# Output gates of a hybrid attention and recurrence block projected in pairs, with the first products of ten pairs moved into the recurrence's stage

## The chip, the cores and the metric

The kernel runs on one core of a Trainium2 chip. The metric is the device time of one execution in microseconds (us), of which the median over three runs is given. The engines are named as in the profile: PE is TensorE's matmul (PEld its weight load), DVE is VectorE, ACT is ScalarE, POOL is GpSimd, and SP is SyncE, which issues the DMA transfers.

## The reference

One layer of an encoder block on a sequence of S = 1024 rows with D = 1024 columns, all in float32. One input projection feeds two mixers; their outputs are merged with gates, and an MLP follows:

```python
proj = x @ w_in
(aq, ak, av, gq, gk, gv, gout, lr_f, lr_b, gate_a, gate_g) = split(proj)
# mixer A: dilated window attention, 3 groups of 4 heads (dilations 1, 4, 16), mixed by their softmax denominators
# mixer B: gated linear attention (GLA), 4 heads, forward and backward over chunks
o_gla = o_gla * rsqrt(mean(o_gla ** 2) + NORM_EPS)
y_gla = o_gla * gla_norm_g * silu(gout)
merged = sigmoid(gate_a) * (y_attn @ w_attn_branch) + sigmoid(gate_g) * (y_gla @ w_gla_branch)
x = layernorm(ALPHA * x + merged @ w_out)
x = layernorm(ALPHA * x + squared_relu(x @ w_ff1 + b_ff1) @ w_ff2 + b_ff2)
```

The part that the change touches is the projection `x @ w_in`. Its columns are cut into 36 blocks of 128 (array `wfm`): 0 to 3 are the recurrence's q and k, 4 to 7 the output gates `gout`, 8 to 23 the two merge gates, 24 to 29 attention's q, 30 to 35 attention's k.

## The kernel before

**Precision.** Every float32 operand is split into a high part, rounded by a copy to the type fp32r, and a low part, the rest. `mm3` (L96) multiplies with three matmuls for each 128 rows of contraction: high by high, high by low, low by high (L100, L101, L102). `load_w` (L87) loads a weight block into a ring of two buffers `raw`, lets ACT make the high part `whi` (L91) and, unless told otherwise, POOL the low part `wlo` (L93). `halve` (L145) does the same for other operands with ACT (L146) and DVE (L147).

**A block alone.** A block of 128 columns times the whole x is two halves of 512 rows, each 8 x 3 = 24 matmuls of 512 columns into one bank of a ring of three (`mmtile`).

**A pair of blocks.** `proj` (L487) computes two blocks at once as a 2 x 2 block product by Winograd's scheme: 7 products of 12 matmuls instead of 8. The sums of x blocks it needs (T1 to T4) are made once by `xsum` (L453) from x loaded anew (`xload`, L448), the sums of weight blocks (S1 to S4) for each pair by `side`. Products are named m1 to m7. m1 (block A11 by B11) leaves its bank as `u2`, a copy by ACT (L547); m2 (A12 by B21) adds to the same bank, which is then the finished first half of the pair's first block; m6, m7, m5, m4, m3 follow, with sums on DVE (L542). Each of the four finished pieces is stored to the DRAM array `spill` by `put` (L519); for attention's q and k this reorders rows by the group's dilation r.

**Order of the stages.** After the start come the recurrence's inputs, and then the recurrence itself: four heads (`gla_head`, L293), each a chain of nine units over PE, ACT, DVE and POOL. `merge_streams` (L58) writes other work between these units: two blocks of q and k, attention's v (`att_v_units`, L422), and the first four half blocks of the output gates (`spill_units`, L403). The other four half blocks stand behind the last head. Then the tiles of the recurrence are given up, T1 to T3 take their place, and T4 takes that of a part of x that is no longer needed. At this handover the sums are made, and between them the products m1 and m2 of the first two pairs run (L618).

After that comes a list of steps, one product each; a step's weight sums are prepared three steps ahead (L816). There are 14 pairs: attention's q and k for groups 2, 1 and 0, then the merge gates. From step 11 on, 27 visits of attention (`visit`, L792) are spread over the steps; the eight `silu` units (L780), which read the stored gates, stand at steps 1 to 8. The merge stage follows, with `load_w` for eight branch weights, and then the output projection, the layer norm and the MLP.

**Who orders the engines.** The program text gives dependencies and priority. A planner in the build (L1546) lays the instructions of each engine in the order in which its own model of time lets them start, earlier text first. On the chip each engine then keeps to that list. So work of different units lies interleaved on PE, and an instruction that is late on the chip holds up what is listed behind it.

## Time and profile before

| What | us |
|---|---|
| median of 3 runs | 1450.34 |
| lowest and highest run | 1446.51 and 1451.52 |
| the profiled execution | 1448.67 |
| its span, first to last instruction | 1446.9 |
| PE busy in it | 1400.9 |
| DVE busy | 994.1 |
| ACT busy | 622.4 |
| POOL busy | 84.6 |

Busy time is the time in which an engine had at least one instruction running. For PE it counts overlapping matmuls once, so it says that the engine was never empty, not how fast it ran. In the rows of the order of time, the first number is the start in us from the span's beginning, the second the duration, then engine, line, operation, output and inputs, and in brackets the idle time before with what ended it. In the rows of waits the three numbers are the total in us, how often, and the longest. In groups, the first number after the bar is the busy time, the second the mean duration in ns. Rows of the windows view give a stretch, its length, the busy time of each engine with the number of instructions, the granted clock of PE, the DMA engines' share and GB/s.

The stages lie about so in the span: start and the recurrence's inputs to 95 us, the four heads to 264 us, the handover to 297 us, the paired projections with attention to 641 us, merge to 710 us, then the rest.

### The profile page before, as it was taken

The numbers are of one execution on the slowest core, as the hardware profiler recorded it, in microseconds if no ns is written. First come the engines' busy times: TensorE is split into PE (matmuls) and PEld (weight loads), VectorE is DVE, ScalarE is ACT, GpSimd is POOL, SyncE is SP. The second block draws the span as 40 slices with busy tenths as digits, with TensorE's granted clock in tenths as the row PEclk, the third lists the DMA queues.
The fourth block names the chain that finished last, engine by engine and source line by source line (L and its number), as shares of the span: only waits on it lengthen the run. The fifth ranks groups of instructions, "written<-read, shape, count | busy, mean of one in ns | idle before, by whom it ended". The sixth has DMA issues, their size and how long they took to land.

```text
span 1446.9 us, 18910 instructions
## 1 busy us (share of the span) xinstructions
PE 1400.9 (97%) x6842; PEld 1167.8 (81%) x6842; DVE 994.1 (69%) x1710; ACT 622.4 (43%) x1180; POOL 84.6 (6%) x67
## 2 busy tenths in 40 slices
PE   8999889989999999999999898999999999999997
PEld 6989887877888888878888676888888888888885
DVE  5155745777555578566646988776666798786988
ACT  5244532434433344345405743555455633433333
POOL 2220312000000000022000000000000000000001
PEclk9999999999999999999999899999999999999999
DMA  7242403495543454275612476854433883544313
GB/s 232 70 132 63 153 31 123 153 280 180 178 144 128 137 165 136 82 231 167 242 58 87 146 243 240 302 170 154 156 139 116 287 331 117 189 131 145 100 47 117
DMA packets 122522, 227.98 MB, mean 158 GB/s; under 512 B 20685, under 2 KB 53709, under 8 KB 122428
## 3 DMA queue, kind: packets, MB, share of 16 engines
q1 hardware_dynamic: 122284, 226.57, 47.4%
q8 instruction: 54, 0.88, 0.3%
q14 instruction: 40, 0.33, 0.1%
q10 hardware_dynamic: 144, 0.20, 0.0%
HBM read 155.32 MB, written 72.44 MB: 157 GB/s over the span
## 4 chain that ended last, share of the span: by engine, by line
PE 86%; DVE 6%; DMA 5%; issue 1%; ACT 1%; SPq 0%; POOL 0%; DVEq 0%; ACTq 0%; POOLq 0%
PE ps L100 16%; PE ps L102 16%; PE ps L101 16%; PE mm L100 10%; PE mm L101 10%; PE mm L102 10%; PE avp L733 3%; DMA x1dr<-res 2%; PE sc L699 2%; PE tr L720 1%; DMA res<-x1dr 1%; PE sc L372 1%; DMA tb<-in_b_ff 1%; DVE T L982 0%; DVE xr L992 0%
## 5 line engine op out<-in xcount | busy, mean ns | idle before, releaser
L93 POOL TENSOR_TENSOR wlo<-raw,whi 128x768 fp32r<-128x768 f32 (+2 forms) x26 | 57.4, 2212 | 505.0 <-ACT whi L91 497.6
L981 ACT CAST T<-hp 128x1024 fp32r<-128x1024 f32 x36 | 37.9, 1052 | 110.0 <-PE ps L101 70.3
L100 PE MATMUL mm<-whi,x 128*128 128x272 f32 (+1 forms) x256 | 81.0, 317 | 0.0
L101 PE MATMUL mm<-wlo,x 128*128 128x272 f32 (+1 forms) x256 | 80.6, 315 | 0.0
L102 PE MATMUL mm<-whi,x 128*128 128x272 f32 (+1 forms) x256 | 80.5, 314 | 0.0
L101 PE MATMUL ps<-B,B 128*128 128x512 f32 x160 | 62.4, 390 | 0.0
L102 PE MATMUL ps<-B,B 128*128 128x512 f32 x160 | 62.3, 389 | 0.0
L100 PE MATMUL ps<-B,B 128*128 128x512 f32 x160 | 61.0, 391 | 0.5 <-ACT B L981 0.5
L100 PE MATMUL ps<-T,fraw 128*128 128x512 f32 x128 | 52.2, 409 | 7.6 <-ACT T L981 5.3
L102 PE MATMUL ps<-B,T 128*128 128x512 f32 x144 | 56.2, 390 | 0.0
L100 PE MATMUL ps<-B,T 128*128 128x512 f32 x144 | 56.2, 390 | 0.0
L102 PE MATMUL ps<-T,T 128*128 128x512 f32 x144 | 56.1, 390 | 0.0
L101 PE MATMUL ps<-T,T 128*128 128x512 f32 x144 | 56.0, 389 | 0.0
L100 PE MATMUL ps<-T,T 128*128 128x512 f32 x144 | 56.0, 389 | 0.0
L101 PE MATMUL ps<-B,T 128*128 128x512 f32 x144 | 56.0, 389 | 0.0
L1360 DVE TENSOR_TENSOR acc<-ps,acc 128x512 f32<-128x512 f32 x68 | 45.8, 689 | 12.9 <-PE ps L102 12.2
L982 DVE TENSOR_TENSOR T<-hp,T 128x1024 fp32r<-128x1024 f32 x36 | 44.0, 1223 | 15.3 <-ACT T L981 15.2
L100 PE MATMUL mm<-x,whi 128*128 128x512 f32 x120 | 47.6, 408 | 6.9 <-ACT x L146 5.8
L709 ACT ACTIVATE e<-e,sm 128x256 f32<-128x256 f32 (+2 forms) x96 | 43.2, 452 | 24.5 <-DVE sm L704 24.4
L101 PE MATMUL ps<-T,fraw 128*128 128x512 f32 x128 | 52.0, 406 | 1.2 <-DVE T L982 1.2
L102 PE MATMUL ps<-T,fraw 128*128 128x512 f32 x128 | 51.5, 404 | 0.0
L542 DVE TENSOR_TENSOR cr<-cu,mm 128x512 f32<-128x512 f32 x42 | 33.7, 805 | 23.2 <-PE mm L102 22.3
(424 smaller groups left out, 4166.5 us busy)
## 6 DMA issues: line engine op xcount, KB each, us to landing
hdr<-c SPq DMA_DIRECT2D x112, 256.0 KB, 2.5
hp<-hdr SPq DMA_DIRECT2D x56, 512.0 KB, 3.7
spill<-cr SPq DMA_DIRECT2D x56, 256.0 KB, 2.6
gate<-spill SPq DMA_DIRECT2D x32, 256.0 KB, 3.0
wa<-in_w SPq DMA_DIRECT2D x16, 512.0 KB, 5.0
wb<-in_w SPq DMA_DIRECT2D x16, 512.0 KB, 6.8
praw<-in_wfm SPq DMA_DIRECT2D x14, 512.0 KB, 4.2
pwhi<-in_wfm SPq DMA_DIRECT2D x14, 512.0 KB, 3.8
```

Of the source, the lines that this page charges most:

```text
L93: (lo_eng or G).tensor_tensor(lo, raw, hi.bitcast(F32), op=OP.subtract)
L100: T.matmul(ps, lh, rh, start=first and i == 0, stop=False, skip_group_check=more)
L101: T.matmul(ps, lh, rl, start=False, stop=False, skip_group_check=more)
L102: T.matmul(ps, ll, rh, start=False, stop=last and i == n - 1, skip_group_check=more)
L372: T.matmul(ap[d][:, i], kd[pr, cs], qd[pr, cs], start=True, stop=True)
L542: V.tensor_tensor(o, a, b, op=OP.add)
L699: T.matmul(sps[i][:, pr, 0:w], q[ps_, pr], k[ps_, pr, 0:w], start=True, stop=True)
L709: issued["exp"] = A.activation(e, e, AF.Exp, bias=sm[:, h:h + 1], scale=-1.0, accum_out=sm[:, 4 + h:5 + h])
L733: T.matmul(av[:, h * 64:h * 64 + 64], b["et"][h % 2][p0:p0 + vv.shape[0], h // 2, j], vv[:, h * 64:h * 64 + 64], start=j == 0, stop=j == n ...
L981: A.copy(o[:, 0], src)
L982: V.tensor_tensor(o[:, 1], src, o[:, 0].bitcast(F32), op=OP.subtract)
L1360: V.tensor_tensor(m, p, m, op=OP.add)
```

## The change

The output gates (blocks 4 to 7) become two more pairs, ahead of the others, so there are 16 pairs and no `spill_units`. For the first ten pairs, m1 and m2 are computed as `first_products`: the first block's weights are loaded whole by `load_w`; the first 12 matmuls give `u2`, which ACT copies and SP stores to a new DRAM array `u2dr`; 12 more accumulate into the same bank, and ACT copies out the finished half, which is stored to `spill`. Eight of the ten stand between the units of the recurrence, two behind. In the steps these ten pairs have five products instead of seven and read `u2` back from DRAM. The products at the handover go. `load_w` uses DVE for the low part everywhere. The ring `stg` gets a fourth buffer, and the `silu` units and attention's visits move behind the first four pairs (`n0` is 20).

```diff
-    def load_w(src, shape, lo_eng=None):
+    def load_w(src, shape):
...
-        (lo_eng or G).tensor_tensor(lo, raw, hi.bitcast(F32), op=OP.subtract)
+        V.tensor_tensor(lo, raw, hi.bitcast(F32), op=OP.subtract)
...
+    u2dr = dr.tile([16, 128, 512], F32, name="u2dr")
...
-    stg = P.open("stg", bufs=3, side="right")
+    stg = P.open("stg", bufs=4, side="right")
...
-    def spill_units(blocks):
...
+    pairs_in = [((b, b + 1), 1) for b in (4, 6)]
+    for g in (2, 1, 0):
+        pairs_in += [((b + 2 * g, b + 2 * g + 1), ORD[g]) for b in (24, 30)]
+    pairs_in += [((b, b + 1), 1) for b in range(8, 24, 2)]
+    NP, EARLY = len(pairs_in), 10
...
+    def first_products(i):
+
+        (b, _), r = pairs_in[i]
+        hi, lo = load_w(io["wfm"][b], [128, KT, 128])
+        w = fm_pairs(hi, lo, 0)
+        ps = mmtile()
+        mm3(ps, w[:4], True, True)
+        o = stg.tile([128, 512], F32, tag="stg", name="u2")
+        A.copy(o, ps)
+        SP.dma_start(u2dr[i], o)
+        mm3(ps, w[4:], False, True, True)
+        o = stg.tile([128, 512], F32, tag="stg", name="h11")
+        A.copy(by_residue(o, r, False), by_residue(ps, r, True))
+        store(b, r, 0, o)
...
-    gout = spill_units(range(4, 8))
-    merge_streams(crit, [lambda: gla_qk("q", 1), lambda: gla_qk("k", 1)] + att_v_units() + gout[:4])
-    for u in gout[4:]:
+    first = [lambda i=i: first_products(i) for i in range(EARLY)]
+    merge_streams(crit, [lambda: gla_qk("q", 1), lambda: gla_qk("k", 1)] + att_v_units() + first[:EARLY - 2])
+    for u in first[EARLY - 2:]:
         u()
...
+        def u2_back():
+            c["u2"] = cu()
+            SP.dma_start(c["u2"], u2dr[n])
+
         s1, s2 = side("S1"), side("S2")
+        if n < EARLY:
+            return dict(raw=raw, steps=[(lambda: (u2_back(), s1(), s2()), [m6]), (side("S3"), [m7]),
+                                        (lambda: None, [m5]), (side("A22"), [m4]), (side("S4"), [m3])])
...
-    for p, n in ((p0, 0), (p1, 0), (p0, 2), (p1, 2)):
-        prep, do = p["steps"][n]
-        prep()
-        for f in do:
-            f()
-    for k in (2, 3):
+    projs[0]["raw"]()
+    projs[1]["raw"]()
+    for k in range(4):
         for nm in ("T1", "T3", "T2", "T4"):
             xsum(nm, k)
+        if k < 2:
+            xload(k + 2)
...
-    a, b = p0["steps"][1], p0["steps"][4]
-    steps = [(a[0], b[1]), p0["steps"][3], (b[0], a[1]), *p0["steps"][5:]] + [p1["steps"][n] for n in (1, 3, 4, 5, 6)]
-    n0 = len(steps)
-    for p in projs[2:]:
-        steps += p["steps"]
+    steps = [st for p in projs for st in p["steps"]]
+    n0 = sum(len(p["steps"]) for p in projs[:4])
...
-        units.setdefault(1 + i, []).append(lambda i=i: silu(i // 2, i % 2))
+        units.setdefault(n0 - 9 + i, []).append(lambda i=i: silu(i // 2, i % 2))
...
-    w = [load_w(io["wo"][1, k2], [128, 2, 512], V) for k2 in range(4)]
+    w = [load_w(io["wo"][1, k2], [128, 2, 512]) for k2 in range(4)]
```

More of the change, by code (lines that the diff above doesn't have):

```diff
@@ L400, in gla_head, with by_residue, store @@
         return units
-    def spill_units(blocks):
-        units = []
-        for wi in blocks:
-            box = {}
-            def half(hf, wi=wi, box=box):
-                if hf == 0:
-                    box["w"] = load_w(io["wfm"][wi], [128, KT, 128])
-                hi, lo = box["w"]
-                ps = mmtile()
-                mm3(ps, fm_pairs(hi, lo, hf))
-                o = stg.tile([128, 512], F32, tag="stg", name="stg")
-                V.tensor_copy(o, ps)
-                SP.dma_start(spill[wi, :, hf * 512:hf * 512 + 512], o)
-            units += [lambda f=half: f(0), lambda f=half: f(1)]
-        return units
+    pairs_in = [((b, b + 1), 1) for b in (4, 6)]
[3 more added lines that the diff above has]
+    NP, EARLY = len(pairs_in), 10
+    def by_residue(a, r, natural):
+        return a.rearrange("p (j c) -> p c j" if natural else "p (c j) -> p c j", c=r)
+    def store(block, r, hf, o):
+        dst = spill[block].rearrange("p (c h j) -> p h c j", h=2, c=r)[:, hf]
+        SP.dma_start(dst, by_residue(o, r, False))
+    def first_products(i):
[11 more added lines that the diff above has]
+        store(b, r, 0, o)
     def att_v_units():
@@ L485, in build, with proj @@
     banks = turns([mmtile() for _ in range(3)], 3)
-    def proj(blocks, r, ahead):
+    def proj(n, ahead):
+        blocks, r = pairs_in[n]
         st, c, ps = {}, {}, {}
@@ L513, in nat, with side @@
         def nat(a):
-            return a.rearrange("p (j c) -> p c j", c=r)
+            return by_residue(a, r, True)
         def stored(a):
-            return a.rearrange("p (c j) -> p c j", c=r)
+            return by_residue(a, r, False)
         def put(f, hf, o):
-            dst = spill[blocks[f]].rearrange("p (c h j) -> p h c j", h=2, c=r)[:, hf]
-            SP.dma_start(dst, stored(o))
-        def side(nm, *ops):
+            store(blocks[f], r, hf, o)
+        def side(nm):
             def f():
@@ L597, in proj @@
                                     (side("S4"), [m3])])
-    todo = []
-    for g in (2, 1, 0):
-        todo += [((b + 2 * g, b + 2 * g + 1), ORD[g]) for b in (24, 30)]
-    todo += [((b, b + 1), 1) for b in range(8, 24, 2)]
-    NP = len(todo)
-    projs = []
-    for i, (bl, r) in enumerate(todo):
-        projs.append(proj(bl, r, (lambda i=i: projs[i + 2]["raw"]()) if i + 2 < NP else None))
-    p0, p1 = projs[:2]
-    p0["raw"]()
-    p1["raw"]()
-    for nm in ("T1", "T3", "T2", "T4"):
-        xsum(nm, 0)
-    xload(2)
-    for nm in ("T1", "T3", "T2", "T4"):
-        xsum(nm, 1)
-    xload(3)
-    for p, n in ((p0, 0), (p1, 0), (p0, 2), (p1, 2)):
-        prep, do = p["steps"][n]
-        prep()
-        for f in do:
-            f()
-    for k in (2, 3):
+    projs = []
+    for i in range(NP):
+        projs.append(proj(i, (lambda i=i: projs[i + 2]["raw"]()) if i + 2 < NP else None))
+    projs[0]["raw"]()
+    projs[1]["raw"]()
+    for k in range(4):
         for nm in ("T1", "T3", "T2", "T4"):
             xsum(nm, k)
+        if k < 2:
+            xload(k + 2)
     P.close("tmp")
@@ L808, in build @@
     for i in range(8):
-        units.setdefault(1 + i, []).append(lambda i=i: silu(i // 2, i % 2))
-    units[n0].append(tiles[0][0]) if n0 in units else units.setdefault(n0, [tiles[0][0]])
+        units.setdefault(n0 - 9 + i, []).append(lambda i=i: silu(i // 2, i % 2))
+    units.setdefault(n0, []).append(tiles[0][0])
     for i in range(3):
```

## Prediction

> **What bounds the kernel now.** I read the page's first two parts, then the windows view by stage, then the waits of PE and the order of time on DVE and POOL where PE waited.
>
> ```profile
> PE 1400.9 (97%) x6842; PEld 1167.8 (81%) x6842; DVE 994.1 (69%) x1710; ACT 622.4 (43%) x1180; POOL 84.6 (6%) x67
> 95.00:264.30 169.30, 158.03 (x952) 143.43 (x950) 95.67 (x136) 68.50 (x160) 35.61 (x24) 0.97 0.28 91
> 264.30:297.00 32.70, 30.22 (x136) 24.69 (x133) 29.41 (x49) 19.08 (x35) 0.00 (x0) 1.00 0.66 203
> 341.00:641.00 300.00, 298.61 (x1597) 244.60 (x1595) 193.65 (x544) 123.79 (x344) 7.39 (x4) 0.99 0.46 146
> ```
>
> The last three rows are the recurrence's stage, the handover to the paired projections, and those projections with attention beside them; their columns are length, PE, PEld, DVE, ACT, POOL, granted clock, DMA share, GB/s. PE is the bound: idle for 1.4 us of the 300, for 2.5 of the 32.7, and for 11.3 only in the recurrence. So what counts is how many matmuls there are, and those few idle places. A matmul's duration is not its cost, because matmuls overlap; the cost is the distance of starts:
>
> ```profile
> 80.42 0.40 PE L100 MATMUL mm<-x,whi 128*128 128x512 f32 x1
> ...
> 97.89 0.40 PE L102 MATMUL mm<-x,wlo 128*128 128x512 f32 x1
> ```
>
> These are the first and last of 78 matmuls without a break: 17.47 us over 77 distances, 0.227 us each, though each is recorded with 0.39. In the Trainium skill, the page "TensorE: Matmul & The Clock Gate", section "Back-to-back issue gap", gives about 131 ns as the sustained spacing at 512 columns. By it the 24 matmuls counted below would be an estimated 3.1 us. The rows decide for 0.227.
>
> The idle places, from the waits of PE in the recurrence (95 to 265 us) and in the handover (265 to 345 us):
>
> ```profile
> PE tr L393 <- DVE on L390: 7.6, 3, 4.6
> PE mm L100 <- ACT stgv L441: 1.1, 1, 1.1
> PE av L382 <- DVE am L374: 1.1, 1, 1.1
> PE sc L303 <- ACT am L373: 0.6, 1, 0.6
> PE tr L338 <- PE tr L393: 0.5, 1, 0.5
> PE sc L303 <- DVE am L374: 0.3, 1, 0.3
> ...
> PE mm L100 <- DVE cu L542: 3.6, 2, 2.5
> ```
>
> Together 11.2 us and 3.6 us. The largest (4.6 us) looks like this on DVE and POOL:
>
> ```profile
> 211.45 2.28 DVE L310 TENSOR_TENSOR_SCAN L<-rmask,zb 64x1024 f32<-64x1024 bf16 x1
> 213.76 2.29 DVE L311 TENSOR_TENSOR_SCAN L<-rmask,zb 64x1024 f32<-64x1024 bf16 x1
> 216.08 0.69 DVE L390 TENSOR_TENSOR on<-av,ss 128x512 f32<-128x512 f32 x1
> ...
> 211.64 2.90 POOL L389 TENSOR_TENSOR ss<-ss,mhalf 128x4 f32<-128x4 f32 x1 [3.34 <-DVE ss L388]
> ```
>
> One head's last norm stands behind the next head's scans, and PE's transposes (L393), queued ahead of ready matmuls, wait for it.
>
> **The change, part by part.**
>
> *Matmuls.* Output gates were 4 blocks x 2 halves x 24 = 192 matmuls; as two pairs of 7 products of 12 they are 168. All else is only moved. So 24 go: 24 x 0.227 = **-5.4 us**. By place: ten first pieces of 24 are 240 where 192 stood in and just behind the recurrence; the 48 of the two pairs' first products at the handover go; the steps fall from 94 to 92.
>
> *Weight splits, POOL to DVE.*
>
> ```profile
> L93 POOL TENSOR_TENSOR wlo<-raw,whi 128x768 fp32r<-128x768 f32 (+1 forms) x10 | 23.3, 2331 | 47.2 <-ACT whi L91 47.2
> ...
> L93 DVE TENSOR_TENSOR wlo<-raw,whi x4: 1225/1226/1227, 722.4 to 730.9; 128x1024 fp32r<-128x1024 f32 x4
> ...
> 150.13 1.84 POOL L93 TENSOR_TENSOR wlo<-raw,whi 128x768 fp32r<-128x768 f32 x1 [23.38 <-ACT whi L91]
> 152.82 1.82 POOL L93 TENSOR_TENSOR wlo<-raw,whi 128x768 fp32r<-128x768 f32 x1 [0.85 <-ACT whi L91]
> ...
> 150.13 1.98 DVE L357 SCALAR_TENSOR_TENSOR S<-S,sm,U 64x128 f32<-64x128 f32 x1
> 152.15 0.74 DVE L360 SCALAR_TENSOR_TENSOR S<-S,sm,U 64x128 f32<-64x128 f32 x2
> 152.92 2.80 DVE L362 TENSOR_TENSOR S<-S,sm 128x1024 f32<-128x1024 f32 x1
> 240.87 1.23 DVE L362 TENSOR_TENSOR S<-S,sm 128x1024 f32<-128x1024 f32 x1
> ```
>
> The same DVE step (L362) takes 2.80 us beside a POOL split and 1.23 alone; the L357 that starts with a POOL split ends with it, at 1.98 us where two of their kind at 152.15 (L360) take 0.74. So DVE pays 1.6 us for a POOL split that meets it, more than the 1.23 us it needs to do one of 1024 columns itself. In 95 to 265 us, ten splits become about 16 (the early pieces double the loads): 16 x at most 1.23 = 20 us on a DVE that is busy 95.67 of 169.30 us, less what the ten meetings cost (0 to 16 us). DVE has room; the recurrence's own chain on it no longer gets the 1.6 us knocks that the planned order did not foresee. New is a wait: a split on DVE stands behind ACT's cast, and the recurrence stands behind the split. I take 4 us off the 11.2 us of stalls, near a third: the scans that carry the largest one stay as they are. Bounds: -11.2 (all go) and +4 (each of the three turns between heads one more split of 1.23 late). Term **-4 us**.
>
> In the Trainium skill, the page "SBUF — State Buffer", section "SBUF: two separate sides", says DVE and GpSimd share a port pair under a lock held for the whole instruction. The rows at 150.13 us agree. By that rule the small power on POOL (L389) stays blocked by DVE's two-input work, of which there is now more; that is rival D.
>
> *More work on ACT, DMA and stores in the recurrence.*
>
> ```profile
> raw<-in_wfm SPq DMA_DIRECT2D x4, 512.0 KB, 4.3
> ...
> L91 ACT CAST whi<-raw 128x768 fp32r<-128x768 f32 (+1 forms) x10 | 9.1, 925 | 9.7 <-issue 3.3 <-DMA raw<-in_wfm 2.5 <-DMA raw<-in_wtv 2.4
> ...
> 225.75 1.05 ACT L91 CAST whi<-raw 128x1024 fp32r<-128x1024 f32 x1 [0.80 <-DMA raw<-in_wfm]
> 278.58 0.58 ACT L547 COPY cu<-mm 128x512 f32<-128x512 f32 x1
> 286.68 0.58 ACT L567 COPY cr<-mm 128x512 f32<-128x512 f32 x1
> ```
>
> A piece asks ACT for 1.05 + 2 x 0.58 = 2.2 us in the 5.4 us of its 24 matmuls; ACT was busy 68.50 of 169.30. Its second half accumulates into the bank that ACT has just copied, so it waits for that copy; three banks and the neighbouring piece cover it. A weight buffer turns over in 4.3 + 1.05 + 1.23 = 6.6 us, two buffers give a piece each 3.3 us, against 5.4 needed: 2.1 us to spare. Each piece adds a load of 512 KB and two stores of 256 KB, about 190 GB/s of its 5.4 us, against 91 GB/s now and 203 in the handover. Term 0, bounds 0 to +5 (half a microsecond for each of ten).
>
> *Handover.* Eight pieces lie between the heads' steps, two behind. Head by head, PE's work in the last head (7 pieces of 5.4 = 38 us plus some 10.5 of its own) equals the 48 us that head takes now (217 to 264 us), so the recurrence should end about where it does. Then the operand sums start:
>
> ```profile
> 264.30:297.00 32.70, 9.96 (x32) 5.89 (x32) 0.00 (x0) 0.00 (x0) 0.00 (x0) 1.00 0.66 203
> L146 ACT CAST xT<-xraw x16: 612/624/632, 265.6 to 287.7; 128x512 fp32r<-128x512 f32 x16
> L147 DVE TENSOR_TENSOR xT<-xraw,xT x16: 685/689/693, 267.0 to 289.0; 128x512 fp32r<-128x512 f32 x16
> ```
>
> The first row is of whi alone: 32 matmuls after 264.3, two of three, so 48 of the gates were left; with the 48 first products, 96 x 0.227 = 21.8 us covered sums that end 25 us later. Now 48 to 96 are left (48 if PE takes all eight pieces first, 240 - 144 = 96 if it runs at today's pace). The sums shrink: four splits and five evacuations leave DVE (9 x 0.6), two weight splits come (2 x 1.2), so some 22 us. PE can also do 27 matmuls (6.1 us) on the first three of four sum slices. Uncovered: 22 - 6.1 - (10.9 to 21.8) = 5 to 0 us; I take 1.6. On the other side stands the 3.6 us wait:
>
> ```profile
> 295.64 0.69 DVE L786 TENSOR_TENSOR et<-et,e 128x512 f32<-128x512 f32 x1 [2.72 <-DMA et<-yodr]
> 296.25 0.68 DVE L542 TENSOR_TENSOR cu<-cu,mm 128x512 f32<-128x512 f32 x1
> ```
>
> A silu unit's product waits 2.72 us for its load, and the sum that PE needs stands behind it. The silu units move to steps 11 to 18, where the DMA crowd of the stage's start is over. Term 1.6 - 3.6 = **-2 us**, bounds -3.6 to +5.
>
> *Steps.* Early pairs have 5 steps with 14 DVE operations instead of 7 with 16; each reads its first sum back:
>
> ```profile
> gate<-spill SPq DMA_DIRECT2D x32, 256.0 KB, 3.0
> 504.00:540.00 36.00, 36.00 (x199) 29.26 (x198) 28.58 (x91) 14.45 (x41) 0.00 (x0) 1.00 0.46 144
> 540.00:576.00 36.00, 36.00 (x208) 29.86 (x207) 29.27 (x94) 16.76 (x48) 0.00 (x0) 1.00 0.49 158
> ```
>
> A transfer of that size lands in 3.0 us and is asked for three steps (8.2 us) ahead. The 27 visits of attention fall on 65 steps instead of 77, 2.41 steps a visit instead of 2.85. At its fullest DVE has 81% now (29.27 of 36); a visit takes about 10.4 us, of which 0.44 x 2.72 = 1.2 us go, and with them about 0.6 us of DVE: 7.8 of 9.2 us, 85%. Still below PE, with less slack: **+1 us**, bounds 0 to +6. The eight splits of the merge stage move to DVE beside 68.58 of 69 us of busy PE: 0.
>
> Sum on the profiled execution: 1448.67 (span 1446.9 and 1.8 around it) - 5.4 - 4 - 2 + 1 = 1438.3. The shown runs' median, 1450.34, is 1.7 above it: **1440 us**.
>
> **Rivals.**
>
> A. *DVE becomes what PE waits for*: splits held up by casts delay the recurrence, and the denser visits delay the steps' sums. For it: 81% already. Against it: 1.4 us idle in 300. It takes the bounds +5 and +6 with no gain elsewhere but the count: 1450.3 - 5.4 + 6 = about 1451, no measurable change. 0.15.
>
> B. *The sums lie bare (slower).* PE takes the pieces wherever the recurrence lets it, and none is left at its end. Then PE waits 25 - 6.1 = 18.9 us at the handover: 1450.3 - 5.4 + 18.9 = 1464. It decides from where 25 - 6.1 - 0.227 n exceeds 5.4, that is under 59 matmuls left if the sums still need 25 us, under 46 if 22. Against it: 96 are left now, and at least 48 are written behind the last head. 0.10.
>
> C. *All stalls of the recurrence go*, with more filling work and a DVE that keeps its planned pace: 1450.3 - 5.4 - 11.2 - 3.6 - 2 for the half clock that follows such gaps = 1428. The clock granted there:
>
> ```profile
> 216.00:252.00 36.00, 33.93 (x178) 27.89 (x179) 19.15 (x30) 11.20 (x26) 11.49 (x5) 0.91 0.35 114
> ```
>
> 0.17.
>
> D. *Only the count stays*: the power on POOL and the norm behind the scans wait as before, no stall goes: 1450.3 - 5.4 = 1445, at the bound of what can be measured. 0.11, half of it on each side.
>
> **How the numbers follow.** The forecast (1434 to 1445) has 0.47. About 0.3% (4.3 us) is what a measurement of this kernel can tell from no change. Faster: 0.47 + 0.17 + 0.05 = 0.69; within: 0.15 + 0.06 = 0.21; slower: 0.10. The range takes in A and C: 1427 to 1452; B is left out.
>
> **What would show it.** PE should have 24 matmuls fewer; POOL no L93; L362 at 1.23 us in every head. The waits of PE for `on` (now L390) should fall from 7.6 us toward 4; over 7.6 speaks for D. An idle place of PE just behind the last transposes of the recurrence, ended by xT's casts or subtracts, is B; its length times 1/0.227 is the cover that lacked. In the steps, waits for cu, cr or the splits of several microseconds are A. The prediction is wrong if the recurrence becomes longer by more than the 48 matmuls it gains.

## The result, and the profile after

The changed kernel takes **1456.91 us** (median of 9 runs) where the kernel before, run beside it, takes 1449.49: a ratio of 1.0051, with a 95% interval of 1.0035 to 1.0067. One run of the changed kernel (2335.68 us, granted clock 0.555) and one of e4 below (1585.57 us, 0.833) are left out of the ratios. The change costs 7.4 us; the forecast was 1440, and its range ended at 1452. The profiled execution took 1456.67 us. The recurrence's lines stand one further down than before: L362 is now L363, L390 is L391, L393 is L394.

The first part of the page, the busy times:

```profile
PE 1406.8 (97%) x6818; PEld 1171.0 (80%) x6818; DVE 1010.4 (69%) x1746; ACT 627.6 (43%) x1184; POOL 24.9 (2%) x41
```

The 24 matmuls are gone (6842 to 6818), and POOL has lost its splits. To see where the time went I cut both spans at the same four places: the recurrence's first matmul (L303, `sc`), its last transposes, attention's first score matmul, the first matmul of the merge. The windows view of the kernel before, cut there:

```profile
79.95:264.30 184.35, 173.08 (x1019) 155.88 (x1017) 105.91 (x144) 77.82 (x174) 38.91 (x26) 0.97 0.31 102
264.30:338.80 74.50, 70.86 (x307) 57.61 (x304) 63.33 (x98) 33.66 (x59) 0.00 (x0) 0.98 0.79 242
338.80:641.60 302.80, 301.04 (x1611) 246.42 (x1610) 196.45 (x552) 125.63 (x346) 7.39 (x4) 0.99 0.46 146
641.60:1446.90 805.30, 781.79 (x3424) 639.59 (x3424) 605.33 (x870) 357.77 (x552) 20.13 (x20) 0.99 0.50 169
```

and of the kernel after:

```profile
80.03:276.68 196.65, 183.41 (x1042) 164.08 (x1040) 109.90 (x155) 88.64 (x190) 10.12 (x14) 0.97 0.37 116
276.68:371.84 95.16, 88.42 (x378) 70.64 (x376) 77.72 (x120) 38.56 (x66) 0.00 (x0) 0.98 0.85 271
371.84:650.60 278.76, 277.15 (x1493) 226.50 (x1492) 187.11 (x544) 114.98 (x327) 0.00 (x0) 0.99 0.49 155
650.60:1454.80 804.20, 782.56 (x3424) 640.65 (x3424) 605.02 (x874) 357.42 (x552) 12.39 (x16) 0.98 0.50 169
```

The recurrence is 12.3 us longer for 24 more matmuls of 512 columns (264 where 240 lay), which cost 24 x 0.227 = 5.4. To compare stages whose work has moved, I take from each length what its big matmuls cost (0.227 us for each of 512 columns; 0.174 for each of 384, the mean distance of their starts at full clock in the kernel before; there are 384 of these in the recurrence, whatever the kernel). What is left, called **excess** below, is the recurrence's own small matmuls, the waits, and the time at half clock. In the recurrence it goes from 63.1 to 70.0 us, at the handover from 6.0 to 10.5, in the steps from 93.7 to 96.6; the part behind is 1.0 us shorter. So +6.9 + 4.5 + 2.9 - 1.0, less 5.4 for the count, is +7.9, the difference of the spans (1446.9 and 1454.8).

Only 2.0 of the recurrence's 6.9 us are idle time of PE: its length less its busy time is 11.3 us before (184.35 - 173.08) and 13.2 after (196.65 - 183.41). In the rest PE is busy, but slower. The clock records show 13.7 us at half clock there where they showed 10.2, and in the kernel after the matmuls of L383 start 0.85 us apart at half clock (220.30, 221.15) where they start 0.45 apart at full clock (214.51, 214.96), so these 3.4 us cost an estimated 1.7. The remaining 3.2 us were not taken apart.

The waits of PE in the kernel after, in the recurrence and at the handover:

```profile
PE tr L394 <- DVE on L391: 7.5, 2, 4.3
PE mm L100 <- ACT stgv L454: 3.6, 1, 3.6
PE mm L100 <- ACT u L426: 1.3, 1, 1.3
...
PE mm L100 <- ACT pwlo L147: 4.1, 2, 2.8
PE mm L100 <- ACT h L430: 1.7, 2, 0.9
PE mm L100 <- ACT u L426: 0.8, 1, 0.8
```

The wait for `on` is still there, 7.5 us where it was 7.6; waits for the copies `u` and `h` are new, and the wait for `stgv` is 3.6 us where it was 1.1. Yet DVE itself is no longer disturbed: the group of the step that took 2.80 us beside a split on POOL is now even in all four heads.

```profile
L363 DVE TENSOR_TENSOR S<-S,sm x4: 1218/1224/1227, 113.6 to 252.5; 128x1024 f32<-128x1024 f32 x4
```

The place with the most idle time is a turn between heads, in the order of time on PE:

```profile
203.82 0.39 PE L100 MATMUL mm<-x,whi 128*128 128x512 f32 x1
...
219.42 1.09 PE L394 MATMUL tr<-ident,on 128*128 128x128 f32 x4 [3.17 <-DVE on L391]
...
225.58 0.39 PE L102 MATMUL mm<-x,wlo 128*128 128x512 f32 x1
230.25 1.09 PE L394 MATMUL tr<-ident,on 128*128 128x128 f32 x4 [4.28 <-DVE on L391]
232.59 0.79 PE L100 MATMUL mm<-x,whi 128*128 128x512 f32 x1 [1.25 <-ACT u L426]
```

on ACT:

```profile
229.00 1.06 ACT L326 ACTIVATE ex<-zb 128x1024 f32<-128x1024 f32 x1
231.38 0.69 ACT L396 ACTIVATE yo<-tr,cols 128x512 f32<-128x512 f32 x1 [1.32 <-PE tr L394]
231.96 0.58 ACT L426 COPY u<-mm 128x512 f32<-128x512 f32 x1
```

and on DVE:

```profile
224.90 2.29 DVE L312 TENSOR_TENSOR_SCAN L<-rmask,zb 64x1024 f32<-64x1024 bf16 x1
227.22 0.17 DVE L389 TENSOR_SCALAR ss<-ss 128x4 f32<-128x4 f32 x1
...
229.41 0.69 DVE L391 TENSOR_TENSOR on<-av,ss 128x512 f32<-128x512 f32 x1 [0.90 <-POOL ss L390]
```

From 203.82 to 225.58 us there are 36 matmuls of the early pieces: three first halves of 12, one in each of the three banks; the third follows the wait of 3.17 us. Then nothing is left to run. The first half is complete at 208 us, but the first copy `u` comes at 231.96, because ACT's list has it behind `yo` (231.38), which waits for the transposes on PE, which wait for DVE's norm, which DVE's list has behind the next head's scans. A bank that takes 24 matmuls before it needs a copy holds twice the work for PE.

This turn was not free before either:

```profile
216.92 1.09 PE L393 MATMUL tr<-ident,on 128*128 128x128 f32 x4 [4.61 <-DVE on L390]
219.16 0.79 PE L100 MATMUL mm<-x,whi 128*128 128x512 f32 x1 [1.15 <-ACT stgv L441]
```

PE idles for 5.8 us there before and for 8.7 after (3.17 + 4.28 + 1.25). So the turn is 2.9 us worse; the recurrence's other waits together are about 1 us shorter.

### The profile page after: what moved, and what is told of

Read it like the earlier page. It is cut to its first block, busy times and chain, and to the rows that moved or that the text cites. A ratio compares the mean times of both kernels' runs of the same rounds, so it can differ in the third digit from the quotient of the medians.

```text
span 1454.8 us, 18923 instructions
## 1 busy us (share of the span) xinstructions
PE 1406.8 (97%) x6818; PEld 1171.0 (80%) x6818; DVE 1010.4 (69%) x1746; ACT 627.6 (43%) x1184; POOL 24.9 (2%) x41
## 4 chain that ended last, share of the span: by engine, by line
PE 71%; DMA 4%; DVE 4%; issue 1%; ACT 1%; DVEq 0%; SPq 0%; ACTq 0%
PE ps L100 16%; PE ps L102 16%; PE ps L101 16%; PE mm L100 6%; PE mm L101 5%; PE mm L102 5%; PE avp L735 3%; PE sc L701 2%; PE tr L722 1%; DMA e<-spill 1%; DMA x1dr<-res 1%; DVE T L982 1%; DMA spill<-cr 1%; DMA tb<-in_b_ff 1%; DVE xr L992 1%
## 5 line engine op out<-in xcount | busy, mean ns | idle before, releaser
L93 DVE TENSOR_TENSOR wlo<-raw,whi 128x1024 fp32r<-128x1024 f32 (+2 forms) x36 | 40.0, 1111 | 68.8 <-ACT whi L91 65.3
L100 PE MATMUL mm<-x,whi 128*128 128x512 f32 x136 | 55.1, 415 | 9.0 <-ACT x L147 4.8
L100 PE MATMUL mm<-xT,pwlo 128*128 128x512 f32 x144 | 58.3, 405 | 4.3 <-ACT pwlo L147 4.1
L100 PE MATMUL ps<-T,fraw 128*128 128x512 f32 x128 | 52.5, 412 | 7.0 <-ACT T L981 5.2
L91 ACT CAST whi<-raw 128x1024 fp32r<-128x1024 f32 (+2 forms) x36 | 34.4, 959 | 57.2 <-PE mm L101 27.9
L101 PE MATMUL mm<-xT,pwlo 128*128 128x512 f32 x144 | 57.2, 397 | 0.0
L102 PE MATMUL mm<-xT,pwlo 128*128 128x512 f32 x144 | 56.5, 393 | 0.0
```

What stands on the lines that cost most here:

```text
L91: A.copy(hi, raw)
L93: V.tensor_tensor(lo, raw, hi.bitcast(F32), op=OP.subtract)
L100: T.matmul(ps, lh, rh, start=first and i == 0, stop=False, skip_group_check=more)
L101: T.matmul(ps, lh, rl, start=False, stop=False, skip_group_check=more)
L102: T.matmul(ps, ll, rh, start=False, stop=last and i == n - 1, skip_group_check=more)
```

## The experiments

Fifteen kernels. "R" is the number of matmuls of 512 columns that lie in the recurrence, "excess" that of recurrence and handover together; ratios are to the kernel before, measured beside each group (medians 1449.6 to 1450.8). The medians are of 4 to 10 runs. e3, e9 and e12 compute another `u2`, and e7 and e8 give other outputs than the kernel after, so these five are read for their times alone.

| run | median us | ratio, 95% | R | excess | steps | behind |
|---|---|---|---|---|---|---|
| before | 1449.49 | 1 | 240 | 69.1 | 93.7 | 805.2 |
| after | 1456.91 | 1.0051 (1.0035 to 1.0067) | 264 | 80.5 | 96.6 | 804.2 |
| e1 | 1456.38 | 1.0035 (1.0021 to 1.0049) | 264 | 77.8 | 97.2 | 804.5 |
| e2 | 1442.07 | 0.9941 (0.992 to 0.9961) | 240 | 69.1 | 92.1 | 799.6 |
| e3 | 1456.69 | 1.004 (1.0023 to 1.0056) | 322 | 78.0 | 97.1 | 804.4 |
| e4 | 1449.61 | 0.9998 (0.9981 to 1.0015) | 264 | 79.5 | 96.7 | 797.4 |
| e5 | 1452.02 | 1.0 (0.9986 to 1.0014) | 192 | 82.4 | 91.6 | 798.8 |
| e6 | 1448.28 | 0.9976 (0.9963 to 0.999) | 240 | 71.8 | 97.4 | 804.7 |
| e7 | 1462.89 | 1.0078 (1.0057 to 1.0099) | 264 | 78.9 | 102.9 | 805.3 |
| e8 | 1461.25 | 1.0072 (1.005 to 1.0095) | 192 | 81.4 | 103.8 | 801.3 |
| e9 | 1448.74 | 0.9987 (0.9972 to 1.0003) | 288 | 80.6 | 94.6 | 800.7 |
| e10 | 1450.68 | 0.9998 (0.9985 to 1.0011) | 240 | 81.4 | 98.8 | 798.5 |
| e11 | 1460.08 | 1.0068 (1.0052 to 1.0084) | 192 | 78.9 | 95.8 | 803.3 |
| e12 | 1445.87 | 0.9972 (0.996 to 0.9985) | 240 | 73.6 | 93.0 | 803.3 |
| e13 | 1447.13 | 0.9986 (0.9973 to 1.0) | 240 | 76.3 | 93.3 | 797.3 |
| e14 | 1453.89 | 1.0013 (0.9998 to 1.0027) | 204 | 80.2 | 95.0 | 803.2 |
| e15 | 1447.94 | 0.9981 (0.9968 to 0.9994) | 252 | 71.6 | 97.1 | 804.5 |

The last four columns come from one profiled execution each. That of e5 lies 3.5 us below its median, that of e10 3.3 above, that of e3 2.3 below, so differences of that size in these columns can belong to the execution.

### The weight splits (e1, e2)

In the kernel after, the splits go back to POOL (e1; those of `w_out` stay on DVE); in the kernel before, all go to DVE (e2).

```diff
 e1, in load_w of after:
-        V.tensor_tensor(lo, raw, hi.bitcast(F32), op=OP.subtract)
+        (lo_eng or G).tensor_tensor(lo, raw, hi.bitcast(F32), op=OP.subtract)
 e2, in load_w of before:
-        (lo_eng or G).tensor_tensor(lo, raw, hi.bitcast(F32), op=OP.subtract)
+        V.tensor_tensor(lo, raw, hi.bitcast(F32), op=OP.subtract)
```

> The changed kernel with the weight splits of load_w back on POOL (those of w_out stay on DVE), nothing else. Theory T (three banks hold first halves whose copies are listed on ACT behind the turn to the last head, so PE runs dry there): about as the changed kernel, 1454 to 1459 us, and PE's idle places between 210 and 235 us stay near 10 us. Rival R1 (the splits on DVE delay the recurrence): 5 us or more less, 1451 or below. Rival R2 (the loss is in the steps, by the moved silu units and the denser attention): as T in time, but the last turn is not what counts.

> The kernel before with all weight splits of load_w on DVE, nothing else. T and R2: within 3 us of the kernel before (1446 to 1452), rather faster, since the DVE steps that met a POOL split (up to 2.80 us) go back to 1.23. R1: slower by 5 us or more, 1454 and up.

Both give the splits nothing. e1 equals the kernel after; but L363 takes 1.23 us in all four heads there too, so no split on POOL meets that step, and it is e2 that decides. e2 is 8.7 us faster than the kernel before beside it, but not where the splits were: its windows for the recurrence, the handover and the part behind the steps are

```profile
80.73:265.27 184.54, 172.84 (x1017) 155.86 (x1016) 107.63 (x156) 78.05 (x174) 12.01 (x14) 0.96 0.32 102
265.27:339.48 74.21, 70.89 (x305) 57.62 (x303) 63.46 (x98) 33.74 (x59) 0.00 (x0) 0.98 0.79 243
...
640.80:1440.30 799.50, 779.37 (x3425) 637.78 (x3423) 604.50 (x875) 357.41 (x552) 12.38 (x16) 0.99 0.50 170
```

The first two rows are those of the kernel before to 0.3 us, with POOL at 12.01 us where it had 38.91; the last is 5.8 us shorter. And its waits of PE there:

```profile
PE tr L393 <- DVE on L390: 9.6, 3, 5.7
```

9.6 us for `on`, against 7.6 before, though L362 takes 1.23 us in all four heads of e2. No split on POOL made the stall at the turns; the rows of the kernel after show the norm behind the next head's scans in DVE's list.

### Where the 5 to 8 us behind the steps come from

In e2 and in e4 (below) nothing of the program text behind the steps differs from a kernel that takes 804 to 805 us there, but for who makes the branch weights' low parts, and that is alike in after and e4. I compared the order of the names and shapes on PE over the last 3424 matmuls. It is the same one in before, after, e1, e3, e6, e7 and e15: 804.2 to 805.3 us. It is a second one in e2, e4 and e5: 797.4 to 799.6. A third one in e11, e12 and e14: 803.2 to 803.3. e8, e9, e10 and e13 each have one of their own (797.3 to 801.3). So the planner lists the output projection and the MLP in another order after an edit far ahead of them, probably since it starts from another state at the end of the steps, and between the first two orders lie 5 to 8 us. The time at half clock does not explain it: among the seven kernels of the first order it runs from 19 to 26 us in that part, and their lengths agree to 1.1 us. Waits of PE in that part are, for instance, in the kernel before around the MLP's first tiles

```profile
PE ps L100 <- DVE c L1126: 1.8, 1, 1.8
PE ps L100 <- ACT fwlo L981: 1.8, 1, 1.8
```

and in e2 in the same stretch

```profile
PE ps L100 <- DVE c L1126: 1.0, 1, 1.0
PE ps L100 <- ACT fwlo L981: 0.9, 1, 0.9
```

This is larger than most of what the experiments test, so from here on the column "excess" is read beside the total.

### The copy in the middle, taken out or moved (e3, e4)

```diff
 e3
-        mm3(ps, w[:4], True, True)
+        mm3(ps, w)
         o = stg.tile([128, 512], F32, tag="stg", name="u2")
         A.copy(o, ps)
         SP.dma_start(u2dr[i], o)
-        mm3(ps, w[4:], False, True, True)
 e4
-        A.copy(o, ps)
+        V.tensor_copy(o, ps)
...
-        A.copy(by_residue(o, r, False), by_residue(ps, r, True))
+        V.tensor_copy(by_residue(o, r, False), by_residue(ps, r, True))
```

> The changed kernel with u2 copied after all 24 matmuls of a piece instead of after 12, so a piece never waits for ACT in its middle and a bank holds 5.4 us of PE's work instead of 2.7 (u2 is then the whole sum, so the three other pieces of these pairs come out otherwise). T: the idle places of the last turn fall from some 10 us to 5 or less, the time by 4 to 7 us, 1450 to 1453. R1 and R2: 1455 to 1458, no change beyond 2 us.

> The changed kernel with both copies of a first piece (u2 and the finished half) on DVE instead of ACT. T, if ACT's list is what holds the banks: 3 to 6 us less than the changed kernel, 1450 to 1454. If DVE at the turn is as tied up by the scans as ACT is by what waits for them: no change within 2 us. R1 (DVE is the short engine): slower, 1459 and up. R2: no change.

With whole pieces (e3) the turn that cost 4.28 us looks like this on PE:

```profile
228.10 0.39 PE L102 MATMUL mm<-x,wlo 128*128 128x512 f32 x1
229.06 0.63 PE L394 MATMUL tr<-ident,on 128*128 128x128 f32 x4 [0.58 <-DVE on L391]
231.43 0.50 PE L100 MATMUL mm<-x,whi 128*128 128x512 f32 x1 [1.74 <-ACT h L429]
```

and on DVE:

```profile
228.24 0.68 DVE L391 TENSOR_TENSOR on<-av,ss 128x512 f32<-128x512 f32 x1
```

From the first piece (203.24 us) to 228.10 there are 72 matmuls, three banks of 24, where the kernel after has 36. The wait for `on` falls from 4.28 to 0.58 us here (in the whole recurrence from 7.5 to 0.6). Of these 3.7 us, 2.5 come from PE, which runs out of work at 228.49 instead of 225.97; 1.2 come from the norm, which is done at 228.92 instead of 230.10, since this listing has it ahead of the scans. So the edit changed the lists as well as the cover. The recurrence's excess falls from 70.0 to 57.9: PE's idle time there from 13.2 to 6.0, and the time at half clock from 13.7 to 3.4 us. But it has taken in 322 matmuls, and the handover has lost that cover:

```profile
79.59:277.27 197.68, 191.72 (x1099) 171.01 (x1098) 113.54 (x160) 90.69 (x193) 9.28 (x14) 0.99 0.41 128
277.27:368.43 91.16, 79.11 (x316) 61.81 (x314) 73.18 (x113) 35.91 (x62) 0.00 (x0) 0.91 0.79 250
```

In the second row PE is busy for 79.11 of 91.16 us. Its waits:

```profile
PE mm L100 <- ACT pwlo L147: 6.7, 1, 6.7
PE mm L101 <- DVE xT L148: 3.3, 2, 1.9
```

The operand sums lie bare, the handover's excess rises from 10.5 to 20.1, and the total stays. e4's seven microseconds are again behind the steps (797.4 against 804.2); its excess is that of the kernel after. Its first copy `u` starts at 232.24 us on DVE, where ACT had it at 231.96: at a turn both engines' lists are full of the head's own chain, so which of them copies does not matter.

### How many pieces lie between the heads (e5, e6)

```diff
-    merge_streams(crit, [lambda: gla_qk("q", 1), lambda: gla_qk("k", 1)] + att_v_units() + first[:EARLY - 2])
-    for u in first[EARLY - 2:]:
+    merge_streams(crit, [lambda: gla_qk("q", 1), lambda: gla_qk("k", 1)] + att_v_units() + first[:4])
+    for u in first[4:]:
```

This is e5; e6 has 6 in the place of 4.

> The changed kernel with four of the ten first pieces written between the recurrence's units and six behind them, instead of eight and two. Theory F (too many pieces stand ahead of the last head's units, and each gives PE only 2.7 us of work before its bank waits for a copy; what is used there is missing as cover of the operand sums): the recurrence ends near 266 us instead of 277, and the time of recurrence and handover beyond their matmuls falls from 80.5 us by 6 or more. Rival H (each turn between heads simply costs what it costs, whatever is written there): recurrence and handover beyond their matmuls stay at 79 or more. The rows behind the merge are listed as in e2 and e4, where that part took 6 to 7 us less than in the changed kernel; so F gives 1441 to 1446, H 1449 to 1452.

> The same with six between and four behind. F: between the changed kernel and four between, the recurrence and handover 3 to 5 us under the 80.5 beyond their matmuls. H: 79 or more.

Six give back 8.7 us of the excess (71.8): 4.1 in the recurrence and 4.7 at the handover, with the copy in the middle as it was. Four give nothing (82.4), where I had expected more from four than from six. Four leave the third turn without a piece: PE waits 2.84 us for `on` there, which before and with six it does not. With six the recurrence holds 240 matmuls, as before.

### Attention's start (e7, e8)

To see whether the steps' 2.9 us come from attention's visits being denser, the output gates' pairs go behind those of groups 2 and 1, so that the visits begin after two pairs instead of four; the `silu` units then share attention's buffers. e8 is the same with four pieces between.

```diff
-    pairs_in = [((b, b + 1), 1) for b in (4, 6)]
-    for g in (2, 1, 0):
-        pairs_in += [((b + 2 * g, b + 2 * g + 1), ORD[g]) for b in (24, 30)]
+    pairs_in = []
+    for g in (2, 1, None, 0):
+        if g is None:
+            pairs_in += [((b, b + 1), 1) for b in (4, 6)]
+        else:
+            pairs_in += [((b + 2 * g, b + 2 * g + 1), ORD[g]) for b in (24, 30)]
...
-    n0 = sum(len(p["steps"]) for p in projs[:4])
+    n0 = sum(len(p["steps"]) for p in projs[:2])
...
-        units.setdefault(n0 - 9 + i, []).append(lambda i=i: silu(i // 2, i % 2))
+        units.setdefault(n0 + 21 + i, []).append(lambda i=i: silu(i // 2, i % 2))
```

> The changed kernel with the two pairs of the output gates behind the pairs of groups 2 and 1 instead of first; attention's visits then start at step 11 as before, spread over 75 steps instead of 65, and the silu units stand at steps 31 to 38. Theory S (part of the loss, some 3 us each, is the denser attention and the silu loads that DVE waits for near 347 us): the idle 2.8 us at 347 us goes, the steps beyond their matmuls go from 96.6 back to 94, the time falls by 3 to 6 us, 1451 to 1454. If the loss lies in recurrence and handover alone: no change beyond 2 us, 1455 to 1459.

> Both: four pieces between and the output gates' pairs later. If F and S both hold their gains add: 1437 to 1443, below the kernel before (about 1450). F alone: as four between. Rows behind the merge listed as in e2 and e4.

Both became slower in the steps (102.9 and 103.8), so this says nothing good of an early start. And e5 and e12, with the visits as dense as in the kernel after, have 91.6 and 93.0, no more than the kernel before (93.7). So density alone is not what costs; over the other runs the steps' excess goes roughly with the time that the clock records show at half speed in them (none in e5, 3.4 us before, 6.8 after, 10.2 in e6). What starts these windows in the steps is left open.

### Six or four between, with other copies (e9, e10, e12)

e9 is e6 with whole pieces as in e3; e12 is e5 with whole pieces; e10 is e6 with both copies on DVE as in e4.

> The kernel after with six pieces between the recurrence's units and four behind, and with u copied once, after all 24 matmuls, instead of in the middle of the piece (u2 is then another number: its 12 matmuls and the other 12 together, so the outputs are others). With eight between, the single copy shortened the recurrence by 12 us and the operand sums at the handover then lay bare. With four pieces behind they should stay covered. Theory H (the bank that an ACT copy must free after each 12 matmuls is what the pieces cost): recurrence and handover together, beyond their matmuls, fall from 71.8 us with six between to 64 or less, so 1442 us or less. Theory F (what counts is how many matmuls the recurrence's gaps get, not when the bank is copied): no change against six between, 1448. If the sums lie bare again, handover over 15 us beyond its matmuls, the copies only hid what the handover costs: 1450 or more.

> The kernel after with six pieces between, and u and h11 copied by DVE instead of ACT. Copies listed on ACT behind the head turn's chain held PE up with eight between, but moving them to DVE did not shorten that recurrence. If the effects add (six between saves 8.7 us at the recurrence and handover, copies by DVE 0 there, and the part behind the merge comes out 7 us shorter because it is listed in another order): 1441. If the shorter part behind the merge was the order that one listing happened to give, and this one gives the longer order: 1448. Theory H2 (it is ACT's place in the list that delays the copies) would give waits of PE for u and h near 0 in the recurrence's tail, and 66 us or less beyond the matmuls.

> The kernel after with four pieces between the recurrence's units and six behind, and u copied once, behind all 24 matmuls (u2 is then another number, so the outputs are others). With eight and with six between, whole pieces left the recurrence's length beyond its matmuls at 58 to 64 us, but the recurrence then took in 82 and 48 more matmuls than before's 240, and the operand sums lay bare (20 and 17 us beyond the matmuls at the handover, 6 before). Theory W (whole pieces cost nothing, and the recurrence has no more room than before filled: what counts is only that some 240 matmuls lie in it and the rest behind): recurrence and handover are again at 69 us beyond their matmuls, before's number, and the time is before's less the count, 1443 to 1446. If the handover stays over 12 us beyond its matmuls, the sums are late for another cause than missing cover: 1449 or more. Theory F (only the turns between heads and their filling count, as with four between and half pieces): 82 us, 1452.

e9 missed what I expected of the middle copy: 48 more matmuls slid into the recurrence (288), the sums lay bare again (handover 17.1), and nothing was won. e10 is no sum of e4 and e6 either: 81.4, and 1450.68 us. e12, however, has the recurrence of the kernel before and more left behind it:

```profile
80.36:265.73 185.37, 173.03 (x1017) 155.47 (x1016) 109.89 (x155) 85.51 (x185) 12.02 (x14) 0.96 0.37 117
265.73:364.70 98.97, 93.99 (x398) 76.22 (x396) 76.96 (x118) 40.65 (x71) 0.00 (x0) 0.97 0.85 268
```

Its excess is 73.6, 8.8 less than e5's, which differs by the middle copy alone, and 1445.87 us is 3.8 below the kernel before beside it. That is the change's count of matmuls (5.4) less 1.6, and just inside what whole pieces were expected to give by the total; by the excess it missed 69.1 by 4.5 us.

### The middle copy alone, in the kernel before (e11, e13)

e11 gives the kernel before one thing of the change: the copy after 12 matmuls, and a store of it that nobody reads. e13 has the same copy and store behind all 24. In both the ring `stg` has a fourth buffer, as in the change.

```diff
 e11
-                mm3(ps, fm_pairs(hi, lo, hf))
+                w = fm_pairs(hi, lo, hf)
+                mm3(ps, w[:4], True, True)
+                o = stg.tile([128, 512], F32, tag="stg", name="u2")
+                A.copy(o, ps)
+                SP.dma_start(u2dr[2 * wi - 8 + hf], o)
+                mm3(ps, w[4:], False, True, True)
 e13
                 mm3(ps, fm_pairs(hi, lo, hf))
+                o = stg.tile([128, 512], F32, tag="stg", name="u2")
+                A.copy(o, ps)
+                SP.dma_start(u2dr[2 * wi - 8 + hf], o)
```

> The kernel before with one thing of the change alone: each of the eight half blocks of the output gates is copied from its bank by ACT after 12 of its 24 matmuls and that first sum is stored to DRAM (nobody reads it), as the change does with u; matmuls, their number and the splits on POOL stay. Theory H (the copy in the middle costs PE about 1 us a piece where the recurrence leaves no other matmuls): 4 to 8 us more than before, 1455 to 1458, in the recurrence and at the handover. Theory F (only the number of filling matmuls and the turns between heads count): within 2 us of before there, 1450.

> The kernel before, its eight half blocks of the output gates with a second copy by ACT and a second store of 256 KB to DRAM (nobody reads it), both behind all 24 matmuls: the work on ACT, its DMAs and the buffer are those of the run with the copy in the middle, and only the break after 12 matmuls is gone. That run took 10.5 us more than before, 9.8 of it in the recurrence and at the handover. If the break is what costs (PE gets 12 matmuls from a bank before it has to wait for a copy, and the second half is listed behind that copy): within 2 us of before, 1449 to 1452. If ACT's time or the stores cost: 1457 or more.

With the middle copy the kernel before takes 10.5 us more, above what either theory gave. Its profiled execution is 12.5 us longer: 9.8 of that are excess, and 2.5 lie ahead of the recurrence, where no such copy stands. The recurrence takes in 48 fewer matmuls (192), 10.9 us of PE, and is only 3.0 us shorter. In e11, PE at the third turn:

```profile
250.75 0.39 PE L384 MATMUL av<-S,q 128*128 128x128 f32 x2
...
251.51 1.16 PE L373 MATMUL sc<-q,k 64*128 64x128 f32 x8
255.50 1.09 PE L394 MATMUL tr<-ident,on 128*128 128x128 f32 x4 [2.83 <-DVE on L391]
256.38 0.64 PE L383 MATMUL av<-gv,am 128*128 128x128 f32 x2
256.81 0.63 PE L384 MATMUL av<-S,q 128*128 128x128 f32 x2
```

and in the kernel before at the same turn:

```profile
255.74 0.40 PE L101 MATMUL mm<-x,whi 128*128 128x512 f32 x1
255.98 0.60 PE L393 MATMUL tr<-ident,on 128*128 128x128 f32 x4
```

There a whole piece fills the turn and the transposes find their operand ready. With the copy in the middle PE waits 2.83 us. The clock records show half clock from 254.2 to 261.1 us, beginning inside this wait: the same pair of L384 takes 0.63 us in place of 0.39. The Trainium skill, page "TensorE: Matmul & The Clock Gate", section "HAM oscillation — how this bites in real kernels", gives as its rule that PE should have no idle gaps of over about 3.4 us; here half clock came with a gap of 2.83. The length of one wait is not all that decides, though: in e6 half clock stands at 463.8 us with no wait over 1.5 us in the 200 us before.

e13 splits the question but does not close it. Its part behind the steps is the shortest of all (797.3), and its excess is 76.3, 7.2 above the kernel before. Of that the recurrence has 2.4, with the same waits at the turns as before; 4.8 lie at the handover, where a piece waits for a bank that DVE copies late, as the waits of PE in e13 show:

```profile
PE mm L100 <- DVE stg L419: 3.2, 1, 3.2
```

So in the recurrence the break costs 5.5 us more than the work of the copy (71.0 against 65.5). At the handover it is the other way round (7.9 with the break, 10.8 without), so of e11's 9.8 us in both, 7.2 are there without the break and 2.6 are the break's. That the total of e13 is below the kernel before, and below the 1449 to 1452 expected, is the part behind.

Four pairs of these runs differ by the break alone. The table gives the excess with the break, then without it.

| pair | recurrence | handover |
|---|---|---|
| eight between: after, e3 | 70.0, 57.9 | 10.5, 20.1 |
| six between: e6, e9 | 65.9, 63.5 | 5.8, 17.1 |
| four between: e5, e12 | 71.6, 64.2 | 10.8, 9.4 |
| kernel before: e11, e13 | 71.0, 65.5 | 7.9, 10.8 |

In the recurrence the break costs in all four, 2.4 to 12.1 us. At the handover three of the four give back 2.9 to 11.3: e3 and e9 since the operand sums lie bare there, e13 with the wait for a bank just shown.

### Two banks instead of one (e14, e15)

```diff
-        mm3(ps, w[:4], True, True)
-        o = stg.tile([128, 512], F32, tag="stg", name="u2")
-        A.copy(o, ps)
-        SP.dma_start(u2dr[i], o)
-        mm3(ps, w[4:], False, True, True)
-        o = stg.tile([128, 512], F32, tag="stg", name="h11")
-        A.copy(by_residue(o, r, False), by_residue(ps, r, True))
+        mm3(ps, w[:4])
+        u = stg.tile([128, 512], F32, tag="stg", name="u2")
+        A.copy(u, ps)
+        SP.dma_start(u2dr[i], u)
+        ps = mmtile()
+        mm3(ps, w[4:])
+        o = stg.tile([128, 512], F32, tag="stg", name="h11")
+        V.tensor_tensor(by_residue(o, r, False), by_residue(u, r, True), by_residue(ps, r, True), op=OP.add)
```

> The kernel after with four pieces between the recurrence's units and six behind, and the two products of a piece in two banks of their own: 12 matmuls, ACT copies u, 12 matmuls in another bank, and DVE adds u and that bank to h11, in place of the second 12 on top of the first in the bank that ACT has just copied. All results are those of the kernel after. Half pieces in one bank gave 1452.0 with four between, whole pieces (one copy) 1445.9. If the cost is the hold of one bank through product, copy, product, copy (the second half listed behind the copy of the first), two banks free PE of it: recurrence and handover at 70 to 75 us beyond their matmuls, 1444 to 1447. If it is that each bank carries 12 matmuls only and has to be emptied every 2.7 us by an engine whose list is held up at the head's turn, nothing changes: 80 to 82 us, 1451 to 1453.

> As the run with four between and two banks, but six between and four behind. Half pieces in one bank gave 71.8 us beyond the matmuls and 1448.3; whole pieces 80.6 and 1448.7, since 48 more matmuls slid into the recurrence and the sums lay bare. If two banks make the pieces as free to slide as whole ones are, the recurrence takes in more than 270 matmuls of 512 columns, the handover is over 13 us beyond its matmuls, and the time is 1448 to 1452. If two banks change nothing against one: 1448, with 240 matmuls in the recurrence.

With four between, two banks give 80.2 where one gave 82.4; with six 71.6 where one gave 71.8. So by these two pairs it does not matter that one bank is held through product, copy, product and copy. What both forms share is that a bank has to be emptied after 12 matmuls.

## Why the prediction was wrong, point by point

| term | predicted | measured in the profiled execution |
|---|---|---|
| count of matmuls | -5.4 | -5.4 |
| recurrence: splits -4, ACT, DMA and stores 0 | -4 | +6.9 |
| handover | -2 | +4.5 |
| steps | +1 | +2.9 |
| part behind | 0 | -1.0 |
| sum | -10.4 | +7.9 |

**The count** was right. The sign that the prediction named for being wrong came: it allowed the recurrence 48 more matmuls (10.9 us), and it is 12.3 us longer for 24.

**"Its second half accumulates into the bank that ACT has just copied, so it waits for that copy; three banks and the neighbouring piece cover it ... Term 0, bounds 0 to +5."** This is the step that failed, and with it "the recurrence should end about where it does": its excess grew by 6.9 us. I weighed ACT's busy time and the weight buffers' turnover as averages over the stage. What the runs show instead is the worst place: at the turn shown above, 24 us pass from the end of the first half (208 us) to its copy (231.96), since the lists hold the recurrence's own work ahead of it, and over that time the three banks give PE 36 matmuls of 0.227 us (8.2 us) instead of 72 (16.3 us). The traces of after and e3 show these counts. The break costs the recurrence 12.1 us as the change has it (after against e3), and 2.4 to 7.4 in the three other pairs, where the bounds were 0 to +5.

That is not the whole of the +11.4 at recurrence and handover. With the break taken out, 8.9 of it stay (e3), now at the handover; with the break left in and six pieces instead of eight between the units, 2.7 stay (e6). So the price of the break depends on how many pieces are listed between the units: two pieces fewer there gave back 8.7 us, the break alone 2.5. Why six half pieces lose so little is not shown.

**The splits, "-4".** DVE's knocks did vanish (2.80 to 1.23 us), and nothing came of it, also where nothing else was changed (e2). They were not on the path: the norm waits behind the scans because the list says so, as rival D had it, and the wait for `on` is 7.5 us after 7.6. D's time, 1445, was 12 us too low, since it too put the pieces at nothing. The Trainium skill, page "SBUF — State Buffer", section "SBUF: two separate sides", has POOL and DVE's two-input work block one another. The power on POOL, which D leans on, became shorter at its longest (2.90 us to 1.84), but DVE waits 5.7 us for it in all where it waited 3.0; at the turn shown above ACT is done with the norm's squares at 224.4 us, L389 starts at 227.22 behind the scans, and DVE then waits 0.90 us for the power. So D was right about the waits, there by the scans' place more than by the power.

**The handover, "-2".** The wait of 3.6 us for `cu` went, as I said. In its place PE waits 4.1 us for `pwlo` and 2.5 for `h` and `u`. The longest, 2.8 us, in the order of time of the kernel after on DVE and PE:

```profile
345.46 0.69 DVE L788 TENSOR_TENSOR et<-et,e 128x512 f32<-128x512 f32 x1 [3.50 <-DMA e<-spill]
...
346.07 0.69 DVE L543 TENSOR_TENSOR psum<-psum,praw 128x512 f32<-128x512 f32 x1
...
347.52 0.50 PE L100 MATMUL mm<-xT,pwlo 128*128 128x512 f32 x1 [2.83 <-ACT pwlo L147]
```

A `silu` unit's product waits 3.50 us for its load, and the weight sum that PE needs stands behind it. The prediction held that mechanism to be gone with the units' move to later steps; it only moved with them. In e7, where these units stand 20 steps later still, the longest wait for `pwlo` at the handover is 1.3 us.

**Rival B**, bare sums, is not what the kernel after shows, but it is real, and e3 and e9 show it (handover 20.1 and 17.1). It is why whole pieces alone do not mend the change: what fills the recurrence is missing behind it. With 240 or 252 matmuls in the recurrence and four or six pieces behind, both have enough: whole pieces in e12 (73.6), half pieces in e6 and e15 (71.8 and 71.6).

**The steps** cost 2.9 instead of 1. I gave it to the visits' density; e5 and e12 speak against that, and it goes with windows at half clock whose cause stays open.

Open is also why six half pieces with copies on DVE (e10) lose 9.6 us more than with copies on ACT (e6), in an execution 3.3 us above e10's median. And the price of the middle copy is from kernels whose lists differ in other places too, as the norm's place in e3 shows; it was not separated from the listing as such.

**Faster than both** is e2, the kernel before with its weight splits on DVE: 1442.07 us, 0.9941 of the kernel before (0.992 to 0.9961). Most of its gain (5.6 of the 6.6 us by which its span is shorter) lies in the part behind the steps, with the order that the planner happens to give it. Of the kernels that make the change, with its results, e15 and e6 are the best (1447.94 and 1448.28), some 0.2% below the kernel before.

## What to carry to other kernels

Ask of filling work not how much there is, but how long the engine can live on it when nobody empties its banks: matmuls per bank times banks, against the longest time in which the copying engines are busy with something else. Work that fills one gap is missing in the next (here two pieces fewer between the heads gave back more than the break taken out), so a stall that goes has to be looked for again where the filler came from. And where a planner orders the lists, compare the order far behind an edit before giving the edit the credit: here the same matmuls in another order were worth as much as the change.

## What the runs showed that I had not expected

An edit in the first 300 us changes the length of a part that starts at 640 us, and whose text is unchanged, by up to 7.9 us (805.2 in before, 797.3 in e13). Kernels with the same order there agree to 2.2 us or better.

Which engine copies a bank made no difference at a turn (231.96 us on ACT, 232.24 on DVE); how many matmuls it held did.

In e11 half clock came with a wait of PE of 2.83 us and lasted for 6.8 us, in which the recurrence's small matmuls take 0.63 us a pair where they take 0.39. So that unfilled turn cost more than its wait.
